# Attention scores on all 128 rows: q stacked high over low, and q padded with zeros

## Chip, cores and metric
The kernel runs on one core of a Trainium2 chip. The metric is the device time of one execution in microseconds (us); lower is better. The engines named below are TensorE (PE; its weight loads are listed apart as PEld), VectorE (DVE), ScalarE (ACT), GpSimd (POOL) and SyncE (SP, which issues the DMAs).

## The reference, cut to what matters
Two blocks of two layers each run one after the other on a sequence of 256 tokens with 1024 columns. Everything is float32. Both blocks contain softmax attention with heads of 64 columns. In the first block 16 query heads share 2 key heads, each query block of 128 tokens sees a band of up to 256 keys, and a sink joins the sum:

```python
def swa_sink_branch(q_in, k_in, v_in, positions, sinks):
    ...
    scores = jnp.einsum('bnqhgd,bnkhd->bnhgqk', qb, kw) * (SW_HEAD_DIM ** -0.5)
    ...
    p = jnp.exp(scores - m)
    probs = p / (jnp.sum(p, axis=-1, keepdims=True) + jnp.exp(sink - m))
    o = jnp.einsum('bnhgqk,bnkhd->bnqhgd', probs.astype(vw.dtype), vw)
```

In the second block there are two streams of 256 tokens, the context stream c and the latent stream h. Each has 6 query heads that share 2 key heads (kind a, `gqa_attention`) and 6 heads with keys of their own (kind b). The latent stream attends to its own keys and to those of the context, 512 in all; in kind b a bias that also holds the mask is added to the scores of its own 256 keys. The last layer computes attention for the latent stream alone.

```python
def gqa_attention(q, k, v):
    ...
        s = jnp.einsum('bqhgd,bkhd->bhgqk', qi, k).astype(jnp.float32) * scale
```

Around the attention stand RMS norms, rotary embedding, a gated delta rule (first block), short convolutions (second block), gates and large feed-forward layers.

## The kernel before
**Matmuls.** Weights stream in by DMA (`wtile`, line 239). Each is split into a high part, rounded to float32r by ACT (line 256), and a low part, the rest, by DVE (line 257). A product is three float32r matmuls: high by high, high by low, low by high (`mm3`, line 260). `lin_a` and `lin_b` loop these over tiles, and `split_psum` (line 229) makes the two parts from a PSUM result. Attention itself runs on plain float32 operands; PE executes such a matmul as two instructions, a weight load with each. Helpers record ACT, DVE tensor and DVE scalar-tensor operations under lines 210, 198 and 201.

**The order of the work.** The program is written as one sequence and a scheduler orders each engine's queue by priority. `weave` (line 566) interleaves softmax groups: three are active, and each round the newest issues its scores, the one before it its transposes, and the oldest its product with the values. `tick` (line 349) spreads the matrix-vector work of the modulation (`ada_steps`, DVE, lines 310 to 324) over other work at a lower priority.

**One softmax group** (`softmax_group`, line 494). Its heads' scores go to one PSUM bank (line 514). DVE finds the maximum (line 520, or with a mask lines 526 and 530), ACT computes the exponentials and their sums (line 538), PE transposes the probabilities (line 551), ACT or DVE copies them out (lines 554, 556), PE multiplies them with the values (line 562), and ACT scales the result (line 564).

**First block** (`attention1`, line 643). After the rotary embedding, the two key heads are each written twice side by side into `kd` (line 659), so that a PE transpose (line 663) puts a copy of the key head into rows 0 to 63 and another into rows 64 to 127 of `kT`. Two query heads lie side by side in 128 columns, so a transpose (line 670) puts the even head into rows 0 to 63 and the odd one into rows 64 to 127 of `qT`; ACT scales by 1/8 as it copies. A score matmul takes one head's 64 rows (line 681). A group holds heads of one parity: four heads by 128 keys for the first token half, two heads by 256 keys for the second.

**Second block.** `mix2` (line 1318) prepares each stream (`prepare`, line 1374): `qk_heads` (line 1234) norms and rotates q and k, then `heads_by_columns` (line 1268) writes `kd`, transposes q (lines 1281 to 1285) and k (lines 1286 to 1291) for both kinds, three heads' pairs at a time. `attend2` (line 1294) builds the groups: two heads with 256 keys each in the context stream, one head with twice 256 keys in the latent stream; heads 0 to 5 of kind a come first, then those of kind b, even and odd in turn. The context stream's groups are woven first, then the latent stream's for both token halves. In the first layer the gate and convolution projections (`conv`, line 1341) are issued before the latent groups, in the last layer after them; the scheduler may draw either forward.

Pools: `ap` holds the attention's tiles (`qT` 2 or 3 buffers, `kT`), `work` holds `w2` (three buffers, shared with evacuations and the modulation), and the PSUM pool for small results has four banks.

Of the kernel before, what the change touches and what calls it, by code (L numbers as in the profile page):

```python
# [9 lines left out]
F32R = mybir.dt.float32r  # L10
# [3 lines left out]
ALU = mybir.AluOpType  # L14
# [3 lines left out]
P = 128  # L18
D = 1024
S = 256  # L20
# [143 lines left out]
class Kern:  # L164
# [329 lines left out]
    def softmax_group(self, ap, heads, sink, out):  # L494


        nc = self.nc
        nh = len(heads)
        nk = sum(p[2] for p in heads[0])
        nb = nk // P  # L500
        biased = heads[0][0][3] is not None
        ncol = len(heads[0]) if biased else 1
        sc = self.t(ap, [P, 512], "sc", bufs=3)
        sc = sc[:, :nh * nk].rearrange("p (h k) -> p h k", h=nh)
        mx = self.t(self.small, [P, nh, 2], "mx", bufs=4)
        nm = self.t(self.small, [P, nh], "nm", bufs=4)
        sums = self.t(self.small, [P, nh, 2], "sums", bufs=4)
        rd = self.t(self.small, [P, nh], "rd", bufs=4)
        ps = self.psum([P, nh, nk])
        src = {}  # L510
        for h, parts in enumerate(heads):
            o = 0
            for i, (q, k, n, bias, _) in enumerate(parts):
                nc.tensor.matmul(ps[:, h, o:o + n], lhsT=q, rhs=k, start=True, stop=True)  # L514
                src[h, i] = (ps[:, h, o:o + n], slice(o, o + n))
                o += n
            if not biased:
                src[h, 0] = (ps[:, h, :], slice(0, nk))
        if not biased:
            nc.vector.tensor_reduce(out=mx[:, :, 0], in_=ps, axis=AX.X, op=ALU.max)  # L520
        else:
            for h, parts in enumerate(heads):
                for i, (_, _, n, bias, _) in enumerate(parts):
                    a, c = src[h, i]
                    if bias is not None:
                        nc.vector.tensor_tensor_reduce(sc[:, h, c], a, bias, scale=1.0, scalar=NEG,
                                                       op0=ALU.add, op1=ALU.max, accum_out=mx[:, h, i:i + 1])
                        src[h, i] = (sc[:, h, c], c)
                    else:
                        nc.vector.tensor_reduce(out=mx[:, h, i:i + 1], in_=a, axis=AX.X, op=ALU.max)  # L530
        other = sink if sink is not None else mx[:, :, 1] if ncol == 2 else None
        if other is not None:
            self.tt(mx[:, :, 0], mx[:, :, 0], other, ALU.max)
        self.ts(nm, mx[:, :, 0], -1.0, ALU.mult)
        for h in range(nh):
            for i in range(ncol):
                a, c = src[h, i]
                self.act(sc[:, h, c], a, AF.Exp, bias=nm[:, h:h + 1], accum_out=sums[:, h, i:i + 1])
        if sink is not None:
            self.tt(sums[:, :, 1], sink, nm, ALU.add)  # L540
            self.act(sums[:, :, 1], sums[:, :, 1], AF.Exp)
        if other is not None:
            self.tt(rd, sums[:, :, 0], sums[:, :, 1], ALU.add)
            nc.vector.reciprocal(rd, rd)
        else:
            nc.vector.reciprocal(rd, sums[:, :, 0])
        yield
        pT = self.t(ap, [P, 4, P], "pT", bufs=2)
        ps = self.psum([P, 4, P])
        for b in range(nh * nb):  # L550
            nc.tensor.transpose(ps[:, b, :], sc[:, b // nb, (b % nb) * P:(b % nb + 1) * P], self.ident)  # L551
        self.flip += 1
        if self.flip % 2:
            nc.scalar.copy(pT[:, :nh * nb, :], ps[:, :nh * nb, :])
        else:
            nc.vector.tensor_copy(pT[:, :nh * nb, :], ps[:, :nh * nb, :])
        yield
        po = self.psum([P, nh, 64])
        for h, parts in enumerate(heads):
            vs = [v for p in parts for v in p[4]]  # L560
            for kb, v in enumerate(vs):
                nc.tensor.matmul(po[:, h, :], lhsT=pT[:, h * nb + kb, :], rhs=v, start=kb == 0, stop=kb == nb - 1)  # L562
        for h in range(nh):
            self.act(out[h], po[:, h, :], scale=rd[:, h:h + 1])

    def weave(self, gens, width, gap=1):

# [74 lines left out]

    def attention1(self, l, ap, swt, oh, ol):
        nc = self.nc
        kT = self.t(ap, [P, 2, S], "kT")
        gens = []
        for tb in range(2):
            x = swt[tb][:, 16:16 + 18 * 64].rearrange("p (h d) -> p h d", d=64)
# [12 lines left out]
            ps = self.psum([P, 4, P])  # L661
            for j in range(2):
                nc.tensor.transpose(ps[:, j, :], kdf[:, j * P:(j + 1) * P], self.ident)
            nc.scalar.copy(kT[:, :, tb * P:(tb + 1) * P], ps[:, 0:2, :])
            qT = self.t(ap, [P, 8, P], "qT", bufs=2)
            for b in range(2):
                ps = self.psum([P, 4, P])
                for j in range(4):
                    c = 16 + (b * 4 + j) * P
                    nc.tensor.transpose(ps[:, j, :], swt[tb][:, c:c + P], self.ident)  # L670
                self.act(qT[:, b * 4:b * 4 + 4, :], ps, scale=0.125)
            o = self.t(self.work, [P, D], "xn", bufs=2)
            nk = P * (tb + 1)
            bias = self.band[:, 0:nk] if tb else self.band[:, P:2 * P]
# [1 line left out]
            for h0 in range(0, 16, step):  # L676
                for par in range(2):
                    hs = range(h0 + par, h0 + step, 2)
                    heads = []
                    for h in hs:  # L680
                        r = slice(par * 64, par * 64 + 64)
                        kv = h // 8
                        vs = [swt[kb][:, 1168 + 64 * kv:1232 + 64 * kv] for kb in range(tb + 1)]
                        heads.append([(qT[r, h // 2, :], kT[r, kv, 0:nk], nk, bias, vs)])
                    c = R_SINK + 16 * l + h0 + par
                    sink = self.rows[:, c:c + step - par:2]
                    gens.append(self.softmax_group(ap, heads, sink, [o[:, 64 * h:64 * h + 64] for h in hs]))
# [579 lines left out]

    def heads_by_columns(self, ap, st, pj, qk, tb, kT):

        nc = self.nc  # L1270
        kd = self.t(ap, [P, 4, 64], "kd")
        for d in range(2):
            nc.vector.tensor_copy(kd[:, d::2, :], qk[:, 6:8, :])
        kdf = kd.rearrange("p a d -> p (a d)")
        qf = qk.rearrange("p h d -> p (h d)")
        s = slice(tb * P, (tb + 1) * P)
        qT = None
        if st.full:
            qT = self.t(ap, [P, 6, P], "qT", bufs=3)
            for b in range(2):  # L1280
                ps = self.psum([P, 3, P])
                for j in range(3):
                    src = qf[:, j * P:(j + 1) * P] if b == 0 else pj[:, 384 + j * P:384 + (j + 1) * P]
                    nc.tensor.transpose(ps[:, j, :], src, self.ident)
                self.act(qT[:, 3 * b:3 * b + 3, :], ps, scale=0.125)
        for j0, m in ((0, 2), (2, 3)):
            ps = self.psum([P, 3, P])
            for j in range(m):
                src = kdf[:, j * P:(j + 1) * P] if j0 == 0 else pj[:, 1024 + j * P:1024 + (j + 1) * P]
                nc.tensor.transpose(ps[:, j, :], src, self.ident)  # L1290
            nc.vector.tensor_copy(kT[:, j0:j0 + m, s], ps[:, :m, :])
        return qT

    def attend2(self, ap, qT, keys, bias, tb):

        o = self.t(self.work, [P, D], "xn", bufs=2)
        heads = {}
        for att in range(2):
            for h in range(6):
                r = slice((h % 2) * 64, (h % 2) * 64 + 64)  # L1300
                kb, v0 = (h // 3, 896 + 64 * (h // 3)) if att == 0 else (2 + h // 2, 1408 + 64 * h)
                parts = []
                for i, (kT, pjs) in enumerate(keys):
                    b = bias[:, h, :] if att == 1 and i == 0 and bias is not None else None
                    parts.append((qT[r, 3 * att + h // 2, :], kT[r, kb, :], S, b, [p[:, v0:v0 + 64] for p in pjs]))
                c = 384 * att + 64 * h
                heads[6 * att + h] = (parts, o[:, c:c + 64])
        per = 2 // len(keys)
# [9 lines left out]
    def mix2(self, l, h, c, nx, then):  # L1318
# [6 lines left out]
        with ExitStack() as es:  # L1325
            xt, ot = nx.x, {}
            with ExitStack() as es2:
# [44 lines left out]
                    ot[st.name] = [self.t(pool, [P, KB, S], tag, F32R, bufs=2) for _ in range(2)]  # L1372

                def prepare(st):
                    kT[st.name] = self.t(ap, [P, 5, S], "kT", bufs=2)
                    for tb in range(2):
                        qk = self.qk_heads(l, ap, st, pj[st.name][tb], tb, True if st is h else None, gtab)
                        qT[st.name, tb] = self.heads_by_columns(ap, st, pj[st.name][tb], qk, tb, kT[st.name])
# [107 lines left out]
```

## Time and profile before

| what | us |
|---|---|
| median of 3 runs | 2934.77 |
| the three runs | 2934.77, 2903.42, 2937.95 |
| the profiled execution | 2933.71 |
| its span, first to last instruction | 2931.9 |
| PE busy in the span | 2863.6 |
| DVE busy | 2110.2 |
| ACT busy | 1320.1 |

The profile is of one execution. Busy time of PE counts from a matmul's start to its modelled end, and matmuls overlap; the distance from one start to the next is the pace. In a timeline a row is one instruction or several alike in a row: start, length, engine, line, operation, written tile and read tiles, shapes, count, and in brackets the idle time before it with what ended it. A form such as 64*128 says that a matmul uses 64 rows and 128 columns of the array. [...]

### The profile page before, as it was taken

What the parts mean: (1) busy time and instruction counts of PE and PEld (TensorE: products, weight loads), DVE (VectorE), ACT (ScalarE), POOL (GpSimd) and SP (SyncE); (2) the same over time, 40 slices, a digit from 0 to 9 for tenths busy, and PEclk for the clock granted to TensorE, in tenths of its full rate; (3) what the DMA queues carried; (4) which work ended last, traced back from release to release, by engine and by line L of the source; (5) the groups of instructions that cost most, each with busy time, mean ns of one, the idle gap of its engine ahead of it and who ended that gap; (6) DMA issues with size and microseconds to landing.
All of it is one profiled execution on the core that took longest, in us unless ns stands there. A gap on an engine that the chain in (4) does not pass through costs nothing.

```text
span 2931.9 us, 51176 instructions
## 1 busy us (share of the span) xinstructions
PE 2863.6 (98%) x19840; PEld 2636.8 (90%) x19840; DVE 2110.2 (72%) x5011; ACT 1320.1 (45%) x2599; POOL 0.2 (0%) x4
## 2 busy tenths in 40 slices
PE   8999999999999999999999999999999999999998
PEld 7999989789988898998978889999999989887897
DVE  7888667988876778777798769777685634764664
ACT  6555464465545554332343555332353323544543
POOL 0000000000000000000000000000000000000000
PEclk9999999999999999999999999999999999987999
DMA  6532557655235665545445224545535433230564
GB/s 221 176 101 73 160 174 236 208 156 172 81 103 171 196 200 170 156 140 154 138 123 160 69 80 125 164 141 154 159 114 160 137 101 107 86 124 12 148 192 143
DMA packets 443908, 416.76 MB, mean 142 GB/s; under 512 B 18320, under 2 KB 383760, under 8 KB 443664
## 3 DMA queue, kind: packets, MB, share of 16 engines
q1 hardware_dynamic: 443664, 413.49, 46.4%
q8 instruction: 156, 2.56, 0.3%
q14 instruction: 88, 0.72, 0.1%
HBM read 412.37 MB, written 1.05 MB: 141 GB/s over the span
## 4 chain that ended last, share of the span: by engine, by line
PE 85%; DVE 7%; DMA 4%; ACT 3%; issue 2%; SPq 0%; DVEq 0%; ACTq 0%
PE mm L265 22%; PE mm L264 22%; PE mm L266 22%; PE sm L514 3%; PE sm L562 3%; DVE lo L198 2%; PE sm L551 2%; DMA araw<-in_w_ada 1%; PE sm L795 1%; DVE acc L201 1%; PE sm L790 1%; ACT hi L210 1%; PE sm L264 1%; PE sm L265 1%; PE sm L266 1%
## 5 line engine op out<-in xcount | busy, mean ns | idle before, releaser
L198 DVE TENSOR_TENSOR lo<-raw,hi 128x1024 fp32r<-128x1024 f32 (+2 forms) x628 | 750.1, 1206 | 339.9 <-ACT hi L210 338.6
L210 ACT ACTIVATE hi<-raw 128x1024 fp32r<-128x1024 f32 (+2 forms) x628 | 647.3, 1046 | 740.0 <-PE mm L265 317.0
L264 PE MATMUL mm<-xTh,hi 128*128 128x256 f32 x2336 | 656.5, 281 | 3.0 <-ACT xTh L210 3.0
L265 PE MATMUL mm<-xTh,hi 128*128 128x256 f32 x2336 | 654.0, 280 | 0.8 <-DVE xTh L201 0.8
L266 PE MATMUL mm<-xTh,lo 128*128 128x256 f32 x2336 | 650.6, 279 | 0.0
L265 PEld LDWEIGHTS mm<-xTh,hi 128*128 128x128 f32 x2336 | 442.9, 190 | 4.7 <-issue 3.3
L264 PEld LDWEIGHTS mm<-xTh,hi 128*128 128x128 f32 x2336 | 438.8, 188 | 5.0 <-ACT xTh L210 3.5
L266 PEld LDWEIGHTS mm<-xTh,lo 128*128 128x128 f32 x2336 | 438.9, 188 | 1.4 <-issue 1.3
L201 DVE SCALAR_TENSOR_TENSOR acc<-araw,csil,acc 128x256 f32<-128x256 f32 x896 | 390.5, 478 | 67.2 <-DMA araw<-in_w_ada 64.7
L264 PE MATMUL mm<-hi,hid 128*128 128x512 f32 x872 | 340.7, 391 | 0.0
L266 PE MATMUL mm<-hi,hid 128*128 128x512 f32 x872 | 340.0, 390 | 0.0
L265 PE MATMUL mm<-lo,hid 128*128 128x512 f32 x872 | 339.7, 390 | 0.0
L264 PE MATMUL mm<-xTc,hi 128*128 128x256 f32 x1104 | 308.9, 280 | 0.0
L265 PE MATMUL mm<-xTc,hi 128*128 128x256 f32 x1104 | 306.6, 278 | 0.0
L266 PE MATMUL mm<-xTc,lo 128*128 128x256 f32 x1104 | 305.3, 277 | 1.1 <-DVE lo L198 1.1
L265 PEld LDWEIGHTS mm<-xTc,hi 128*128 128x128 f32 x1104 | 208.6, 189 | 0.7 <-issue 0.3
L266 PEld LDWEIGHTS mm<-xTc,lo 128*128 128x128 f32 x1104 | 206.5, 187 | 1.3 <-DVE lo L198 1.3
L264 PEld LDWEIGHTS mm<-xTc,hi 128*128 128x128 f32 x1104 | 206.6, 187 | 0.3
L266 PEld LDWEIGHTS mm<-hi,hid 128*128 128x128 f32 x872 | 164.0, 188 | 34.3
L264 PEld LDWEIGHTS mm<-hi,hid 128*128 128x128 f32 x872 | 164.0, 188 | 33.2
L265 PEld LDWEIGHTS mm<-lo,hid 128*128 128x128 f32 x872 | 163.9, 188 | 33.3 <-DVE lo L198 0.2
L264 PE MATMUL mm<-hi,xTh 128*128 128x256 f32 (+3 forms) x512 | 178.3, 350 | 4.4 <-ACT xTh L1147 2.8
(315 smaller groups left out, 4631.7 us busy)
## 6 DMA issues: line engine op xcount, KB each, us to landing
raw<-in_ffn_wi SPq DMA_DIRECT2D x352, 256.0 KB, 3.7
araw<-in_w_ada SPq DMA_DIRECT2D x288, 256.0 KB, 3.0
raw<-in_w_ff SPq DMA_DIRECT2D x128, 512.0 KB, 4.2
raw<-in_w_in SPq DMA_DIRECT2D x116, 512.0 KB, 4.0
raw<-in_ffn_wo SPq DMA_DIRECT2D x88, 512.0 KB, 4.1
raw<-in_w_o SPq DMA_DIRECT2D x40, 512.0 KB, 3.3
raw<-in_w_in SPq DMA_DIRECT2D x24, 432.0 KB, 4.6
raw<-in_w_up_sw SPq DMA_DIRECT2D x16, 512.0 KB, 3.6
```

Source lines behind the costliest of these rows:

```text
L198: self.nc.vector.tensor_tensor(out=out, in0=a, in1=b, op=op)
L201: self.nc.vector.scalar_tensor_tensor(out=out, in0=a, scalar=s, in1=b, op0=op0, op1=op1)
L210: self.nc.scalar.activation(out, a, func, **kw)
L264: mm(ps, lhsT=ah, rhs=bh, start=first, stop=False)
L265: mm(ps, lhsT=ah, rhs=bl, start=False, stop=False)
L266: mm(ps, lhsT=al, rhs=bh, start=False, stop=last)
L514: nc.tensor.matmul(ps[:, h, o:o + n], lhsT=q, rhs=k, start=True, stop=True)
L551: nc.tensor.transpose(ps[:, b, :], sc[:, b // nb, (b % nb) * P:(b % nb + 1) * P], self.ident)
L562: nc.tensor.matmul(po[:, h, :], lhsT=pT[:, h * nb + kb, :], rhs=v, start=kb == 0, stop=kb == nb - 1)
L790: nc.tensor.matmul(ps[:, i, :], lhsT=LT[:, i, :], rhs=Dm[:, i, :], start=True, stop=True)
L795: nc.tensor.matmul(ps[:, i, :], lhsT=DT[:, i, :], rhs=M[:, i, :], start=True, stop=True)
```

## The change
Heads that share keys (all of the first block, kind a of the second): a new helper, `stack_q`, writes each head's q as a stack of 128 rows, the float32r high part in its own 64 rows and the low part in the other 64. The keys, already present in both halves, are split into `kh` and `kl` (float32r). A score is then two accumulating float32r matmuls over 128 rows, the stack times `kh` and the stack times `kl`. Heads with keys of their own (kind b): q goes into `qz`, a tile of 128 rows in which GpSimd fills the other head's 64 rows with zeros; the score is one float32 matmul of 128 rows against the pair of key heads in `kb`. `kd` is now written after the q transposes and takes a buffer of `w2`. Edits that only renumber the entries of a part are left out.

```diff
@@ softmax_group
-            for i, (q, k, n, bias, _) in enumerate(parts):
-                nc.tensor.matmul(ps[:, h, o:o + n], lhsT=q, rhs=k, start=True, stop=True)
+            for i, (qk, n, bias, _) in enumerate(parts):
+                for m, (q, k) in enumerate(qk):
+                    nc.tensor.matmul(ps[:, h, o:o + n], lhsT=q, rhs=k, start=m == 0, stop=m == len(qk) - 1)
...
+    def stack_q(self, qs, ps, scale):
+        for d in range(2):
+            own, other = slice(64 * d, 64 * d + 64), slice(64 - 64 * d, 128 - 64 * d)
+            self.act(qs[own, d::2, :], ps[own], scale=scale)
+            self.stt(qs[other, d::2, :], ps[own], scale, qs[own, d::2, :], ALU.mult, ALU.subtract)
...
@@ attention1
-        kT = self.t(ap, [P, 2, S], "kT")
+        kh, kl = (self.t(ap, [P, 2, S], x, F32R) for x in ("kh", "kl"))
...
-            nc.scalar.copy(kT[:, :, tb * P:(tb + 1) * P], ps[:, 0:2, :])
-            qT = self.t(ap, [P, 8, P], "qT", bufs=2)
+            s = slice(tb * P, (tb + 1) * P)
+            self.split_psum(kh[:, :, s], kl[:, :, s], ps[:, 0:2, :])
+            qs = self.t(ap, [P, 16, P], "qs", F32R, bufs=2)
...
-                self.act(qT[:, b * 4:b * 4 + 4, :], ps, scale=0.125)
+                self.stack_q(qs[:, b * 8:b * 8 + 8, :], ps, 0.125)
...
-                        r = slice(par * 64, par * 64 + 64)
...
-                        heads.append([(qT[r, h // 2, :], kT[r, kv, 0:nk], nk, bias, vs)])
+                        qk = [(qs[:, h, :], k[:, kv, 0:nk]) for k in (kh, kl)]
+                        heads.append([(qk, nk, bias, vs)])
...
@@ heads_by_columns
-        kd = self.t(ap, [P, 4, 64], "kd")
-        for d in range(2):
-            nc.vector.tensor_copy(kd[:, d::2, :], qk[:, 6:8, :])
-        kdf = kd.rearrange("p a d -> p (a d)")
+        kh, kl, kb = kT
...
-            qT = self.t(ap, [P, 6, P], "qT", bufs=3)
+            q = self.t(ap, [P, 6, P], "qs", F32R, bufs=3), self.t(ap, [P, 2, 3, P], "qz", bufs=3)
+            for d in range(2):
+                nc.gpsimd.memset(q[1][64 - 64 * d:128 - 64 * d, d], 0.0)
...
-                self.act(qT[:, 3 * b:3 * b + 3, :], ps, scale=0.125)
+                if b == 0:
+                    self.stack_q(q[0], ps, 0.125)
+                else:
+                    for d in range(2):
+                        r = slice(64 * d, 64 * d + 64)
+                        self.act(q[1][r, d], ps[r], scale=0.125)
+        kd = self.t(self.work, [P, 4, 64], "w2", bufs=3)
+        for d in range(2):
+            nc.vector.tensor_copy(kd[:, d::2, :], qk[:, 6:8, :])
+        kdf = kd.rearrange("p a d -> p (a d)")
...
-            nc.vector.tensor_copy(kT[:, j0:j0 + m, s], ps[:, :m, :])
-        return qT
+            if j0 == 0:
+                self.split_psum(kh[:, :, s], kl[:, :, s], ps[:, :m, :])
+            else:
+                nc.vector.tensor_copy(kb[:, :, s], ps[:, :m, :])
+        return q
...
@@ attend2
-                    parts.append((qT[r, 3 * att + h // 2, :], kT[r, kb, :], S, b, [p[:, v0:v0 + 64] for p in pjs]))
+                    qk = [(qT[0][:, h, :], k[:, h // 3, :]) for k in kT[:2]] if att == 0 else [(qT[1][:, h % 2, h // 2, :], kT[2][:, h // 2, :])]
+                    parts.append((qk, S, b, [p[:, v0:v0 + 64] for p in pjs]))
...
@@ mix2, prepare
-                    kT[st.name] = self.t(ap, [P, 5, S], "kT", bufs=2)
+                    kT[st.name] = [self.t(ap, [P, 2, S], x, F32R, bufs=2) for x in ("kh", "kl")] + [self.t(ap, [P, 3, S], "kb", bufs=2)]
```

## Rows read from the trace of the kernel before

**Rows 1.** The page: busy time by engine, and the chain of waits by engine.
```profile
PE 2863.6 (98%) x19840; PEld 2636.8 (90%) x19840; DVE 2110.2 (72%) x5011; ACT 1320.1 (45%) x2599; POOL 0.2 (0%) x4
...
PE 85%; DVE 7%; DMA 4%; ACT 3%; issue 2%; SPq 0%; DVEq 0%; ACTq 0%
```
**Rows 2.** Table by stage: length, busy PE, PEld, DVE, ACT, POOL, granted clock, DMA.
```profile
50.00:97.00 47.00, 46.97 (x337) 40.04 (x335) 37.84 (x163) 33.64 (x118) 0.00 (x0) 1.00 0.39 115
614.00:661.00 47.00, 46.99 (x344) 40.72 (x342) 39.78 (x174) 34.34 (x121) 0.00 (x0) 1.00 0.41 124
1608.00:1641.00 33.00, 32.28 (x218) 26.49 (x216) 19.94 (x67) 19.89 (x76) 0.00 (x0) 1.00 0.08 29
1672.00:1750.00 78.00, 77.87 (x456) 62.16 (x456) 55.06 (x178) 42.24 (x122) 0.00 (x0) 1.00 0.29 91
2620.00:2677.00 57.00, 55.59 (x199) 44.70 (x199) 19.27 (x70) 18.08 (x58) 0.00 (x0) 0.50 0.11 33
```
**Rows 3.** The scores' line: instructions, ns min/median/max, and matmuls of each form.
```profile
L514 PE MATMUL sm<-kT,qT x368: 272/376/792, 51.4 to 2703.1; 64*128 64x256 f32 x152, 64*128 64x128 f32 x32
```
**Rows 4.** PE's timeline, first block's attention in the second layer.
```profile
631.42 1.00 PE L562 MATMUL sm<-swt,pT 128*128 128x64 f32 x8
632.35 1.13 PE L514 MATMUL sm<-kT,qT 64*128 64x256 f32 x4
633.41 0.39 PE L265 MATMUL mm<-xTh,hi 128*128 128x256 f32 x1
633.64 0.28 PE L266 MATMUL mm<-xTh,lo 128*128 128x256 f32 x1
633.76 0.28 PE L264 MATMUL mm<-xTh,hi 128*128 128x256 f32 x1
```
**Rows 5.** PE's timeline: 128-column scores, and float32 of 128 rows in the delta rule.
```profile
614.59 1.71 PE L514 MATMUL sm<-kT,qT 64*128 64x128 f32 x16
...
260.79 2.12 PE L771 MATMUL sm<-kq 128*128 128x256 f32 x8
262.75 0.50 PE L795 MATMUL sm<-M,DT 128*128 128x128 f32 x3
```
**Rows 6.** PE's timeline, last layer's latent attention: front, one round, end.
```profile
2614.70 1.14 PE L514 MATMUL sm<-kT,qT 64*128 64x256 f32 x8
...
2617.67 0.66 PE L551 MATMUL sm<-cst,sc 128*128 128x128 f32 x4 [1.40 <-ACT sc L210]
2618.26 1.13 PE L514 MATMUL sm<-kT,qT 64*128 64x256 f32 x4
...
2621.73 2.07 PE L514 MATMUL sm<-kT,qT 64*128 64x256 f32 x4
2623.74 1.11 PE L551 MATMUL sm<-cst,sc 128*128 128x128 f32 x4
2624.64 1.81 PE L562 MATMUL sm<-pj,pT 128*128 128x64 f32 x8
2626.38 2.07 PE L514 MATMUL sm<-kT,qT 64*128 64x256 f32 x4
...
2674.12 1.11 PE L551 MATMUL sm<-cst,sc 128*128 128x128 f32 x4 [1.41 <-ACT sc L210]
...
2677.87 1.13 PE L514 MATMUL sm<-kT,qT 64*128 64x256 f32 x4
```
**Rows 7.** Groups of instructions by line and shape: count, busy us, mean ns.
```profile
L201 DVE SCALAR_TENSOR_TENSOR xTh<-sm,hg,xTh 128x512 fp32r<-128x512 f32 x8 | 5.4, 741 | 0.0
L210 ACT ACTIVATE qT<-sm 128x384 f32<-128x384 f32 x12 | 5.2, 488 | 1.3 <-PE sm L1284 1.3
L526 DVE CUSTOM_DVE_ANT_0 sc<-sm,bias 128x256 f32<-128x256 f32 x24 | 10.2, 425 | 26.6 <-PE sm L514 26.5
L210 ACT ACTIVATE sc<-sc,nm 128x256 f32<-128x256 f32 x56 | 28.1, 504 | 18.6 <-DVE rd L544 10.0 <-DVE nm L205 8.4
```
**Rows 8.** PE's timeline, front of the context stream: first transposes after the scores.
```profile
1611.47 0.44 PE L551 MATMUL sm<-cst,sc 128*128 128x128 f32 x2 [0.72 <-ACT sc L210]
```

More of the change, by code (lines that the diff above doesn't have):

```diff
@@ L498, in softmax_group @@
         nh = len(heads)
-        nk = sum(p[2] for p in heads[0])
+        nk = sum(p[1] for p in heads[0])
         nb = nk // P
-        biased = heads[0][0][3] is not None
+        biased = heads[0][0][2] is not None
         ncol = len(heads[0]) if biased else 1
@@ L522, in softmax_group @@
             for h, parts in enumerate(heads):
-                for i, (_, _, n, bias, _) in enumerate(parts):
+                for i, (_, n, bias, _) in enumerate(parts):
                     a, c = src[h, i]
@@ L559, in softmax_group @@
         for h, parts in enumerate(heads):
-            vs = [v for p in parts for v in p[4]]
+            vs = [v for p in parts for v in p[3]]
             for kb, v in enumerate(vs):
@@ L1270, in heads_by_columns @@
         nc = self.nc
-        kd = self.t(ap, [P, 4, 64], "kd")
-        for d in range(2):
-            nc.vector.tensor_copy(kd[:, d::2, :], qk[:, 6:8, :])
-        kdf = kd.rearrange("p a d -> p (a d)")
+        kh, kl, kb = kT
         qf = qk.rearrange("p h d -> p (h d)")
         s = slice(tb * P, (tb + 1) * P)
-        qT = None
+        q = None
         if st.full:
-            qT = self.t(ap, [P, 6, P], "qT", bufs=3)
+            q = self.t(ap, [P, 6, P], "qs", F32R, bufs=3), self.t(ap, [P, 2, 3, P], "qz", bufs=3)
+            for d in range(2):
+                nc.gpsimd.memset(q[1][64 - 64 * d:128 - 64 * d, d], 0.0)
             for b in range(2):
@@ L1299, in attend2 @@
             for h in range(6):
-                r = slice((h % 2) * 64, (h % 2) * 64 + 64)
-                kb, v0 = (h // 3, 896 + 64 * (h // 3)) if att == 0 else (2 + h // 2, 1408 + 64 * h)
+                v0 = 896 + 64 * (h // 3) if att == 0 else 1408 + 64 * h
                 parts = []
```

## The prediction
> **What bounds the kernel now.** I read the busy times and the chain of waits first: TensorE (PE) is busy 98% of the span and carries 85% of the chain [rows 1]. [...] Five stretches hold the attention scores (line 514): the first block's attention in both layers (50 to 97 and 614 to 661 us), the second block's context stream (1608 to 1641) and latent stream (1672 to 1750) in its first layer, and the latent stream in its second (2620 to 2677, with a rest up to 2704). In all of them PE is 97 to 100% busy, so PE is the bound; but in the first block's two, VectorE (DVE) is busy 37.8 and 39.8 of 47 us, close behind. And one differs: from 2620 to 2677 the granted clock is 0.50 (1.2 GHz), in the others 1.00 (2.4 GHz) [rows 2].
>
> The times are those of the profiled execution: span 2931.9, with 1.8 us around it 2933.7. The median of the three runs is 2934.8, so terms can be taken from it directly. One of the three is 2903.4, 31 us shorter; I come back to that.
>
> **One block of scores.** There are 184 score matmuls, and each float32 one is two instructions, 368 in all, on 64 of the 128 rows; 152 of the matmuls have 256 columns, 32 have 128 [rows 3]. In the timeline a block of four (one round's scores) starts at 632.35 and the next matmul at 633.41: 1.06 us. That next one, a float32r matmul of 128 rows, is followed only 0.23 later by its successor, where this form then runs at 0.12 (633.64 to 633.76): the change of form costs another 0.11. A block costs 1.17 [rows 4].
>
> **The change, heads with shared keys** (all 64 score matmuls of the first block, 60 of the second's 120). Two float32r instructions of 128 rows replace two float32 instructions of 64: the same count. At 0.115 to 0.12, four make 0.47, and 0.09 for entering float32r after a float32 or transpose block (taken a little below the 0.11 above) 0.56. A 256-column block saves 1.17 - 0.56 = 0.6 us. Of 128 columns the trace has no float32r matmul. The float32 ones of 128 columns, at the front of a first-block attention, took 1.71 for 16, 0.107 each [rows 5]. Below, 0.115 is the pace of 64-column float32 matmuls, 0.93 for eight [rows 4], which looks like a floor per weight load; above, 0.245 is the pace of a float32 instruction with 128 rows and 256 columns, eight from 260.79 to 262.75 [rows 5]. I take 0.115, the row nearest in width: no gain or loss. At the upper end 32 per layer would cost 32 x 0.13 = 4.2 us a layer.
>
> **Heads with own keys** (60 matmuls). They stay float32 and get 128 rows, half of them zeros. At 0.245 [rows 5] four make 0.98 against 1.17: 0.2 saved, all of it change of form.
>
> **What is lost.** At the front of the last attention eight score instructions take 1.14 (2614.70), as long as four elsewhere [rows 4, 6]: two groups on opposite row halves ran side by side. Two such fronts are as good as unchanged (8 x 0.115 = 0.92), so I drop about 1 us at each front. [...]
>
> PE's saving by stage: first block, eight 256-column groups a layer, 8 x 0.6 and some 0.7 of changes of form, 5.5 a layer; context stream 6 x 0.6 + 6 x 0.2 - 1 = 3.8; latent stream, first layer, 12 x 0.6 + 12 x 0.2 - 1 = 8.6; second layer, the ten groups after 2677, 4 x 0.6 + 6 x 0.2 = 3.6.
>
> **The added work.** stack_q makes of one ACT evacuation two and adds two DVE operations (stt). From the nearest row, an stt from PSUM to float32r of 128x512 at 0.741 [rows 7]; with 384 columns, by share, 0.56. The stacked tiles have 64 partitions; the records here show cost by columns, so I take the full price (half of it is the lower bound). First block: 4 x 2 x 0.741 and two subtractions for k of half the columns, some 0.4 each, give DVE 6.7 us a layer. There DVE had 7 to 9 us free of 47 [rows 2], and PE's part shrinks to 41.5: DVE, 44.5 to 46.5, is then the longer one, unless its modulation work slips out of the stretch. So of 5.5 I take 1.5 a layer, 3 for both (bounds -1 and 5.5 a layer).
> In the second block three preparations get, per token half, 2 x 0.56 of DVE and two more ACT evacuations of 0.49 [rows 7]; kh and kl replace one DVE copy by an ACT copy and a subtraction. The second token half's keys release the first scores. In their way come about 1.1 (DVE), 0.5 and 0.4 (ACT): 2 us per stage, of which projection matmuls cover a little: -5 in all (bounds 0 and -8). Each new stt also waits some 0.5 for ACT's copy; behind it in DVE's queue stand the subtractions that split weights, for which the covering projection matmuls wait: part of the same 5. The 12 zero fills go to GpSimd, which has nothing else (4 instructions, [rows 1]); their price isn't in the trace, but the tile is wanted several us later; I take nothing. If a fill took 2 us, it would still be under the chain of norm, rope and transposes. kd, now behind the q transposes and in one of three shared buffers, delays k by the stacking already counted.
>
> **The half-clock stretch** is the largest term. The clock fell after the block at 2618.26 (1.13, still 2.4 GHz) and before that at 2621.73 (2.07); just ahead PE had idled 1.40 us (before 2617.67). It stayed at 1.2 GHz through eleven rounds like the one shown, each with a 64-row block of 2.0 us. It was at 2.4 GHz again in the block at 2677.87 (1.13), after some 6 us without a 64-row block: transposes, value matmuls and an idle of 1.41 [rows 6]. A full-clock round needs 1.06 + 0.59 (transposes, 2617.67 to 2618.26) + 0.93 = 2.58 [rows 4, 6]; here it is 4.65 (2621.73 to 2626.38). I read it as: the 64-row blocks keep the clock down once a gap has lowered it. The change leaves none. A fall at the front is then still likely (the first exponentials are no faster), but it should be brief.
> New stage, from 2614.70 to 2677.87 (63.2 now; a front of two groups up to 2618.26, twelve rounds, a tail of some 3.6): front 3.6 as now; six shared-key rounds, 0.56 + 0.59 + 0.93 = 2.1 each; between a group's scores and its transposes the trace has 1.83 (2615.84 to 2617.67) [rows 6], which PE's other work just covers. Six own-key rounds: PE 2.5; their chain is longer, mask and maximum 0.43 each and two exponentials of 0.50 [rows 7], with small steps and semaphores some 2.6: 2.6 each. Tail 2, a brief half clock 2.5. Sum 3.6 + 12.6 + 15.6 + 2 + 2.5 = 36, saved 27.
>
> **Sum.** 3 (first block) + 2/3 of 16 (3.8 + 8.6 + 3.6; the rest goes into waits for the softmax), 11, + 27 - 5 = 36: 2933.7 - 36 = **2898 us**. Against the run of 2903 it would be a gain of 5 only; I suspect that this run kept its clock, since the stage at full clock would be 3.6 + 12 x 2.6 + 2 = 37, and 63.2 - 37 = 26 is most of the 31.
>
> **Rivals.**
> 1. *The clock stays low in the last stage* (it also falls where chains idle, and transposes and value matmuls remain). Then, with 0.90 and 1.74 for transposes and value matmuls [rows 6] and the scores at twice their time, rounds cost 0.94 + 0.09 + 0.90 + 1.74 = 3.7 and 1.96 + 0.90 + 1.74 = 4.6; stage 3.6 + 22.2 + 27.6 + 3.6 = 57, saved 6: 2933.7 - (3 + 11 + 6 - 5) = 2919. For it: PE is quicker, so idles longer. Against: the recovery at 2677 needed only the instructions that remain.
> 2. *All of PE's saving is real* and preparation is covered: 11 + 16 + 29.5 (no brief half clock): 2877. Against: DVE in the first block.
> 3. *Slower: the clock falls in the context stream too.* Its front has the same shape and now less PE work to bridge the first exponentials; before, PE idled 0.72 there [rows 8], after, about 1.5 with preparation longer. It decides from a gap like the 1.40 that preceded the fall. Twelve rounds at about 4.1 instead of 2.5, some 20 us, and as much again in part of the latent stream (10), with the last stage as in rival 1: 2919 + 30 = 2949. Against: projection matmuls stand between the rounds there.
> 4. *The half clock is chance, not the rows*: some runs have it, some not, before and after. Then the median may fall on either side, 2898 or 2919.
>
> **How the numbers follow.** Forecast 0.54, rival 1 0.17, rival 2 0.16, rival 3 0.06, rival 4 0.07. The range, 2870 to 2926, takes in the 128-column price, DVE's bounds and rivals 1 and 2, and leaves out rival 3 and the far ends. A measurement of this kernel can tell about 2% (58.7 us) from no change. Faster by more, below 2876, needs rival 2 with a little more: 0.17; slower by more, 2993, needs rival 3 in more than two stages: 0.03; within 0.80.
>
> **What would show it.** Right: no 64-row form at line 514; shared-key blocks of four near 0.47 and own-key blocks near 0.98; a clock of 1.00 in most of the last stage and its length near 36; DVE above 90% in the first block's attention. Wrong: a clock of 0.50 through that stage, or 128-column instructions near 0.245, or new PE idle at each stage's front of over 3 us.

## The result and the profile after

The kernel after takes 2884.78 us (median of four runs, 2882.61 to 2889.78); the kernel before, run beside it, 2933.13 (2903.42 to 2937.95). The ratio is 0.9864, 95% interval 0.9816 to 0.9912: 1.4% faster. The profiled execution took 2885.26 us, its span is 2883.5. The forecast of 2898 was 13 us too long, and its range holds the result.

The page, where [rows 1] stood: the count of PE's instructions is the same, PE is 59 us less busy, DVE and ACT a little more; POOL's 12 added zero fills took 5.0 us.

```profile
PE 2804.2 (97%) x19840; PEld 2608.6 (90%) x19840; DVE 2131.3 (74%) x5043; ACT 1333.5 (46%) x2627; POOL 5.2 (0%) x16
...
PE 82%; DVE 9%; DMA 4%; ACT 4%; issue 2%; SPq 0%; DVEq 0%; ACTq 0%
```

The table by stage, where [rows 2] stood (length, busy PE, PEld, DVE, ACT, POOL, granted clock, DMA):

```profile
50.00:97.00 47.00, 45.17 (x377) 43.01 (x375) 44.06 (x176) 36.87 (x126) 0.00 (x0) 1.00 0.40 120
614.00:661.00 47.00, 42.63 (x350) 41.36 (x351) 43.08 (x175) 37.08 (x128) 0.00 (x0) 0.96 0.39 118
1604.00:1636.00 32.00, 32.00 (x261) 31.20 (x260) 24.88 (x85) 21.55 (x78) 0.82 (x2) 1.00 0.17 54
1664.00:1740.00 76.00, 73.14 (x480) 63.54 (x481) 60.50 (x197) 43.46 (x121) 0.00 (x0) 0.98 0.36 112
2598.00:2635.00 37.00, 33.22 (x248) 28.87 (x246) 26.28 (x89) 22.93 (x69) 0.00 (x0) 1.00 0.23 72
```

Two things are to be seen. In the first block's two stretches PE is no longer full: 1.8 and 4.4 us of 47 idle, with DVE at 44.1 and 43.1. And the last stretch is at a clock of 1.00 and is 37 us long where it was 63. The 0.96 of the second layer is a short fall that is new: PE idled 1.86 us at the front there, the clock was at 0.50 from 621.6 to 625.0, and then at 1.00 again.

```profile
621.16 0.33 PE L552 MATMUL sm<-cst,sc 128*128 128x128 f32 x1 [1.86 <-ACT sc L210]
```

The scores' line, where [rows 3] stood: no 64-row form is left.

```profile
L515 PE MATMUL sm<-kh,qs x124: 273/283/455, 53.1 to 2641.9; 128*128 128x256 f32 x92, 128*128 128x128 f32 x32
...
L515 PE MATMUL sm<-kb,qz x120: 377/379/435, 1608.7 to 2657.6; 128*128 128x256 f32 x120
```

PE's timeline of the last layer's latent attention, where [rows 6] stood: front, shared-key rounds, an own-key round.

```profile
2598.61 0.39 PE L515 MATMUL sm<-kh,qs 128*128 128x256 f32 x1 [0.36 <-ACT kh L210]
...
2602.14 0.27 PE L266 MATMUL mm<-xTh,lo 128*128 128x256 f32 x1
2602.62 0.66 PE L552 MATMUL sm<-cst,sc 128*128 128x128 f32 x4 [0.20 <-ACT sc L210]
2603.03 0.36 PE L515 MATMUL sm<-kh,qs 128*128 128x256 f32 x1
...
2603.59 0.60 PE L552 MATMUL sm<-cst,sc 128*128 128x128 f32 x4
...
2605.07 0.36 PE L515 MATMUL sm<-kh,qs 128*128 128x256 f32 x1
...
2606.09 0.66 PE L552 MATMUL sm<-cst,sc 128*128 128x128 f32 x4 [0.29 <-ACT sc L210]
...
2607.39 0.36 PE L515 MATMUL sm<-kh,qs 128*128 128x256 f32 x1
...
2610.64 0.66 PE L552 MATMUL sm<-cst,sc 128*128 128x128 f32 x4 [0.55 <-ACT sc L210]
...
2611.97 1.08 PE L515 MATMUL sm<-kb,qz 128*128 128x256 f32 x4
2613.21 0.66 PE L552 MATMUL sm<-cst,sc 128*128 128x128 f32 x4 [0.15 <-ACT sc L210]
...
2614.54 1.08 PE L515 MATMUL sm<-kb,qz 128*128 128x256 f32 x4
...
2634.93 0.36 PE L515 MATMUL sm<-kh,qs 128*128 128x256 f32 x1
```

At the front, projection matmuls now run until 2602.4, so PE idles 0.20 us before the first transposes, not 1.40, and the clock stays at 1.00 through this stage. Three shared-key rounds (2605.07 to 2611.97) take 2.3 each, with 0.3 to 0.55 us in two of them in which PE waits for the exponentials; the one own-key round shown takes 2.57, of which 0.15 is such a wait.

Where the time went, from the start of the first score instruction to the start of the last in each stage, by five of the profiles (the last three columns are kernels of the experiments):

| stage, us | before | after | all 64 rows | all padded | first block padded |
|---|---|---|---|---|---|
| first block, layer 1 | 43.5 | 40.3 | 47.1 | 38.4 | 38.4 |
| first block, layer 2 | 42.6 | 41.1 | 49.5 | 38.2 | 38.2 |
| context stream | 29.1 | 28.2 | 32.1 | 26.0 | 28.2 |
| latent, first layer | 73.6 | 70.0 | 77.2 | 66.8 | 68.5 |
| latent, last layer | 88.4 | 59.0 | 71.1 | 60.0 | 59.0 |
| sum | 277.1 | 238.6 | 277.1 | 229.3 | 232.3 |

The stages give 38.5 of the 48 us between the two spans. The four stretches between them sum to 2374.5 before and 2365.9 after, but a second profile of the kernel before, taken in the experiments, has 2366.8: in sum those 9 us are mostly what the same kernel varies by.

### The profile page after: what moved, and what is told of

Read it like the earlier page. It is cut to its first block, busy times and chain, and to the rows that moved or that the text cites. A ratio compares the mean times of both kernels' runs of the same rounds, so it can differ in the third digit from the quotient of the medians.

```text
span 2883.5 us, 51232 instructions
## 1 busy us (share of the span) xinstructions
PE 2804.2 (97%) x19840; PEld 2608.6 (90%) x19840; DVE 2131.3 (74%) x5043; ACT 1333.5 (46%) x2627; POOL 5.2 (0%) x16
## 4 chain that ended last, share of the span: by engine, by line
PE 82%; DVE 9%; DMA 4%; ACT 4%; issue 2%; SPq 0%; DVEq 0%; ACTq 0%
PE mm L265 22%; PE mm L264 22%; PE mm L266 22%; PE sm L563 2%; DVE lo L198 2%; PE sm L515 2%; DVE acc L201 2%; PE sm L552 1%; DMA araw<-in_w_ada 1%; PE sm L805 1%; PE sm L800 1%; ACT hi L210 1%; PE sm L264 1%; PE sm L265 1%; PE sm L266 1%
```

## The experiments

**All scores on 64 rows again.** Stacking, splitting and padding stay, but each matmul reads its head's own 64 rows (the low part of q, and the zeros, are left out of the products).

```diff
-    qk = [(qs[:, h, :], k[:, kv, 0:nk]) for k in (kh, kl)]
+    r = slice(h % 2 * 64, h % 2 * 64 + 64)
+    qk = [(qs[r, h, :], k[r, kv, 0:nk]) for k in (kh, kl)]
```

(and the same in `attend2`, for both kinds.)

> The changed kernel with all its added work, but every score matmul takes only the 64 rows of its own head (for shared keys the low part of q, which lies in the other 64 rows, is left out of the scores). Theory A (blocks on 64 rows keep the clock down once a gap has lowered it): the last latent stage is at a clock of 0.50 for most of its rounds, some 55 us long instead of 35, and each block costs 0.1 to 0.2 us more for the change of form; 2912 to 2922 us. Rival B (the clock depends on the idle gap at the stage's front and on PE's pace, both as in the changed kernel here, not on rows): clock 1.00 there, 2885 to 2900 us. Rival C (chance): runs of either kind in one kernel.

Measured 2924.54 (2913.76 to 2930.39), ratio 1.001 [0.9977, 1.0043], just above theory A's 2912 to 2922. With the rows the whole gain goes, float32r or not. It was not only the clock: its run of 2913.76 had a mean granted clock of 0.993, like the kernel after, and is still some 29 us above it. What theory A said of the clock did not come in the run that was traced: PE idled only 0.37 us at the last stage's front, and 33 us of rounds with 64-row blocks ran at 1.00 before 17 us at half clock:

```profile
2632.00:2665.00 33.00, 31.03 (x211) 25.43 (x211) 22.45 (x79) 19.95 (x59) 0.00 (x0) 1.00 0.23 72
2665.00:2682.00 17.00, 16.18 (x61) 13.33 (x61) 6.09 (x17) 5.19 (x14) 0.00 (x0) 0.51 0.00 1
```

So 64-row blocks alone did not lower the clock in those 33 us, behind a front idle of 0.37 us.

**Only the own-key heads on 64 rows.** The same edit for kind b alone.

> The changed kernel, but the heads with own keys take only their own 64 rows (nothing is left out: the other rows hold zeros). Theory A: blocks of these heads cost 1.06 to 1.17 again instead of 0.73 to 0.92, and if a gap in the own-key half of the last latent stage lowers the clock there, it stays at 0.50 to that half's end: 2888 to 2905 us. Rival B: clock 1.00 throughout, only the change of form, 2887 to 2893 us.

Measured 2896.88 (2890.65 to 2900.93), ratio 0.9899: 8 us above the kernel after as repeated below, 12 above its first median. For 30 blocks that is 0.26 to 0.40 a block; the prediction had 0.2. By stage its profile gives less: context stream, latent stream and last layer take 30.7, 70.7 and 61.5 us, against 28.2, 68.5 and 59.0 in the second profile of the kernel after, 7.2 in all or 0.24 a block.

**Padding alone.** The kernel before, with q of every head padded with zeros to 128 rows in the manner of `qz`, one float32 matmul each, and no stacking.

```diff
-    qT = self.t(ap, [P, 8, P], "qT", bufs=2)
+    qT = self.t(ap, [P, 2, 8, P], "qT", bufs=2)
+    for d in range(2):
+        nc.gpsimd.memset(qT[64 - 64 * d:128 - 64 * d, d], 0.0)
...
-    heads.append([(qT[r, h // 2, :], kT[r, kv, 0:nk], nk, bias, vs)])
+    heads.append([(qT[:, par, h // 2, :], kT[:, kv, 0:nk], nk, bias, vs)])
```

> The kernel before, with q of every head padded with zeros to 128 rows; scores stay float32, no split, no stacking (GpSimd fills, ACT evacuates twice). PE has the pace of before and the same front with its idle gap, only the rows differ. Theory A: clock back at 1.00 within a few us of the last latent stage's front, stage of 36 to 40 us, and 0.1 to 0.3 us less per block: 2893 to 2905 us. Rival B (gap and pace decide): clock 0.50 in that stage as before, 2915 to 2930 us. Rival C: either, from run to run.

Measured 2880.50 (2878.59 to 2882.82), ratio 0.9851 [0.9797, 0.9904]: at least as fast as the change, and below the 2893 to 2905 expected, without float32r scores and without the 21 us of DVE work. The table by stage of this kernel shows where:

```profile
614.00:661.00 47.00, 46.98 (x382) 45.55 (x382) 42.46 (x157) 34.04 (x112) 0.00 (x0) 1.00 0.41 122
```

PE is full there, as before [rows 2], but in the same 47 us it issues 382 instructions where the kernel before issued 344 and the kernel after 350. At the last stage's front the idle was not the same as before, as the expectation had it, but half as long:

```profile
2592.86 0.66 PE L551 MATMUL sm<-cst,sc 128*128 128x128 f32 x4 [0.74 <-ACT sc L210]
```

The eight score instructions took 1.96 us there and not 1.14, which fills part of the old idle, and the clock stayed at 1.00 (every later block of the stage took 1.03 to 1.08). So this run prices the 64 rows, but does not show what they do to a clock that has fallen.

**The kernel before, again.**

> The kernel before, unchanged, to see its runs one by one. Theory A: runs near 2933 us have a mean clock near 0.984, a run near 2903 (if one comes) near 0.994, the difference being the half-clock stretch of the last latent stage. Rival C the same, and then in about a third of the runs. If a run near 2903 came with a clock of 0.984, its 31 us are something else.

Measured 2930.61, ratio 1.0018. In the experiments the kernel before ran 59 times, these ten included, and its runs fall in two groups: 26 of 2903 to 2917 us, with a mean granted clock of 0.990 to 0.996, and 33 of 2927 to 2953, with 0.977 to 0.987. Both traced runs are of the second group. In the first profile of the kernel before, the half-clock stretch lasts 58 us (2619.6 to 2677.6), which alone lowers the mean clock of a 2932 us run by 0.010: without it, that run's 0.984 would be 0.994, as in the first group. By this estimate, the stretch is there in somewhat more than half of the runs. The run traced here (2946.87, clock 0.978) has it twice:

```profile
2614.00:2656.00 42.00, 42.00 (x148) 33.54 (x149) 14.20 (x57) 14.06 (x47) 0.00 (x0) 0.50 0.10 29
...
2662.45 0.66 PE L551 MATMUL sm<-cst,sc 128*128 128x128 f32 x4 [1.41 <-ACT sc L210]
...
2665.00:2713.00 48.00, 48.00 (x154) 36.68 (x152) 13.52 (x51) 13.54 (x42) 0.00 (x0) 0.50 0.00 0
```

The clock came back in between (1.00 from 2657 to 2662), after transposes and value matmuls of two rounds had run with no 64-row block between them. It fell again behind an idle of 1.41 us.

Of the kernels with 128 rows, 36 runs (the change and the padded ones, all but the one that stacks twice) all had 0.991 to 0.997.

**First block padded, second as in the change; and the reverse.** The first block takes the edit above, the second keeps the stack; then the other way about.

> The changed kernel, but the first block's attention keeps float32 scores with q padded by zeros to 128 rows, in place of the stacking (no split of its k, no stt); the second block is as in the change. If the stacking of the first block costs what it saves or more because DVE is the longer engine there, this is 5 to 12 us below the changed kernel: 2873 to 2880 us. If float32r's pace pays in the first block, it is 5 to 11 us above: 2890 to 2896 us.

> The other half: first block stacked as in the change, second block with zeros and float32 for all heads. If the stacking in the second block pays (its PE time 0.56 a block against 0.92, 30 blocks, less the longer preparation), this is 3 to 8 us above the changed kernel: 2888 to 2893 us. If its preparation costs as much as it saves: 2883 to 2887 us. Padding everywhere stood at 2880.5 us, so this and the run with the first block padded should lie on opposite sides of it or add up to it: first block's step plus second block's step = -4.

**The change with each subtraction of the stack issued twice,** and **the change again,** on the same chip:

```diff
     self.stt(qs[other, d::2, :], ps[own], scale, qs[own, d::2, :], ALU.mult, ALU.subtract)
+    self.stt(qs[other, d::2, :], ps[own], scale, qs[own, d::2, :], ALU.mult, ALU.subtract)
```

> The changed kernel with every stt of stack_q issued twice (same result): 28 more DVE operations, 16 of 0.684 and 12 of 0.555, 17.6 us of DVE. If the added DVE work stands on the path in the first block and in the preparations, 8 to 15 us above the changed kernel: 2893 to 2900 us. If it is hidden behind matmuls: within 3 us of it.

> The changed kernel, unchanged, beside the three others on the same chip: 2880 to 2890 us, mean clock 0.992 to 0.995 in every run. A run with a clock near 0.984 would say that the half-clock stretch can come without blocks on 64 rows.

Measured: change again 2889.18; first block padded 2875.62 (ratio 0.9852 [0.9801, 0.9903]), 13.6 less; second block padded 2890.08, 0.9 more; stack twice 2903.84, 14.7 more. In the first block the stack loses to padding; twice the stacking lengthens the kernel by about its added DVE time (17 us by the page). So DVE is on the path there. Part of the 14.7 is clock: the runs that stack twice had 0.985 to 0.991, and the one at 0.991 (2901.39) stands 12 above the change's at 0.991. PE's timeline of that kernel shows how the two hang together, in the first block and at the last layer's front:

```profile
657.21 0.44 PE L552 MATMUL sm<-cst,sc 128*128 128x128 f32 x2 [0.99 <-ACT sc L210]
...
660.70 0.56 PE L552 MATMUL sm<-cst,sc 128*128 128x128 f32 x2 [1.51 <-ACT sc L210]
...
2617.94 1.12 PE L552 MATMUL sm<-cst,sc 128*128 128x128 f32 x4 [2.30 <-ACT sc L210]
```

and its table by stage, around the two:

```profile
660.00:680.00 20.00, 17.38 (x81) 16.71 (x82) 13.30 (x50) 9.42 (x35) 0.00 (x0) 0.52 0.39 115
2617.00:2630.00 13.00, 11.94 (x55) 11.65 (x56) 8.94 (x21) 5.67 (x17) 0.00 (x0) 0.50 0.13 42
```

After idles of 0.99 and 1.51 us, and of 2.30, the clock fell to 0.50, and with 128-row blocks and further idles among them it was back 13 to 20 us later. That suggested the next pair.

**An idle forced at the front of the last layer's latent attention,** in the padded kernel and in the kernel before:

```diff
-    nc.vector.tensor_reduce(out=mx[:, :, 0], in_=ps, axis=AX.X, op=ALU.max)
+    for _ in range(8 if getattr(self, "lag", 0) > 0 else 1):
+        nc.vector.tensor_reduce(out=mx[:, :, 0], in_=ps, axis=AX.X, op=ALU.max)
+    self.lag = getattr(self, "lag", 0) - 1
...
+    self.lag = 2 if last else 0
     self.weave(gens, 3)
```

> The kernel before with q padded to 128 rows for every head (no stacking), and at the front of the last layer's latent attention the maximum of the first two groups taken 8 times instead of once (7 more of 0.69 us each, 4.8 us a group), so that TensorE must idle there for some 4 to 9 us. Theory (an idle lowers the clock, and only rounds with 64-row blocks keep it down): granted clock 0.50 after the idle for some 10 to 15 us (as in the run that stacks twice, where it fell after an idle of 2.30 and was back 13 us later), then 1.00 for the rest of the stage; 9 for the idle and 6 for the clock over the padded kernel's 2880: about 2895 (2888 to 2902). Rival (the rows do not matter; once fallen, the clock stays down through any stage of this kind): 0.50 to the stage's end, about 2880 + 9 + 25 = 2914.

> The kernel before with the same idle forced at the same place; scores on 64 rows. Theory: the clock falls at this front in every run, not only in some, and stays at 0.50 through the rounds with 64-row blocks, some 55 us; so no run near 2905, all of them 2935 to 2950. Rival (a fall is chance, an idle does not bring it): times as scattered as those of before, 2905 to 2950, each some 9 later.

Measured: padded with idle 2888.06 (2885.87 to 2890.06); before with idle 2943.86, no run of ten below 2940.41, while the kernel before beside them had ten of 17 runs under 2912. Timeline of the padded kernel with idle:

```profile
2584.20 1.95 PE L514 MATMUL sm<-kT,qT 128*128 128x256 f32 x8
...
2595.44 1.12 PE L553 MATMUL sm<-cst,sc 128*128 128x128 f32 x4 [9.06 <-ACT sc L210]
2596.35 1.92 PE L514 MATMUL sm<-kT,qT 128*128 128x256 f32 x4
...
2600.00 1.08 PE L514 MATMUL sm<-kT,qT 128*128 128x256 f32 x4
...
2602.57 1.08 PE L514 MATMUL sm<-kT,qT 128*128 128x256 f32 x4
2603.49 0.60 PE L553 MATMUL sm<-cst,sc 128*128 128x128 f32 x4
2603.93 1.00 PE L564 MATMUL sm<-pj,pT 128*128 128x64 f32 x8
2604.77 1.08 PE L514 MATMUL sm<-kT,qT 128*128 128x256 f32 x4
```

and of the kernel before with idle:

```profile
2611.73 1.14 PE L514 MATMUL sm<-kT,qT 64*128 64x256 f32 x8
...
2623.01 1.12 PE L553 MATMUL sm<-cst,sc 128*128 128x128 f32 x4 [9.71 <-ACT sc L210]
2624.06 2.07 PE L514 MATMUL sm<-kT,qT 64*128 64x256 f32 x4
...
2688.91 2.07 PE L514 MATMUL sm<-kT,qT 64*128 64x256 f32 x4
...
2693.21 1.05 PE L553 MATMUL sm<-cst,sc 128*128 128x128 f32 x4
2694.20 1.13 PE L514 MATMUL sm<-kT,qT 64*128 64x256 f32 x4
```

with its table by stage:

```profile
2623.00:2693.00 70.00, 68.58 (x235) 54.02 (x236) 24.39 (x84) 21.45 (x67) 0.00 (x0) 0.50 0.09 27
```

The idle was as long in both (9.06 and 9.71). With 128 rows the block at 2596.35 ran at half clock (1.92) and the one at 2600.00 at full (1.08): 5 us after the idle it was over. With 64 rows blocks took 2.07 for 65 us, with PE busy 98% of the time, and 1.13 again from 2694.20, after 2.3 us of projection matmuls (five float32r of 128 rows, left out in the rows). The same shows once more, without a forced idle, near the end of the stage. The kernel before fell behind an idle of 1.41 us and stayed low for the 48 us shown above. The padded kernel with idle fell behind one as long, and its block at 2634.63 was at full clock again:

```profile
2629.27 0.66 PE L553 MATMUL sm<-cst,sc 128*128 128x128 f32 x4 [1.41 <-ACT sc L210]
...
2634.63 1.08 PE L514 MATMUL sm<-kT,qT 128*128 128x256 f32 x4
```

So behind idles of 9.06 and 9.71 us the clock was low in both kernels, for 5 us with 128-row blocks and for 70 with 64-row ones; both halves of the prediction's reading are shown for this stage. The rival, a fall that stays whatever the rows, is refuted. The number of rows in use and the change of form around each 64-row block went together in all these kernels, so which of the two keeps the clock low is not shown. What lets the kernel before keep its clock in the other runs, a shorter idle at this front or something else, was not traced.

The padded kernel with idle is 5.5 us above the padded one beside it (2882.61, below), not the 15 expected, though its last stage is 11.0 us longer (71.0 and 60.0). Where the rest was made up is open.

**Padded everywhere against first block only,** side by side on one chip:

> q padded for every head, a second time, to stand beside the next kernel on the same chip. 2880 as before if chips agree. If stacking pays in the second block (two float32r instructions at 0.115 for two float32 ones at 0.245), the next kernel is faster by 60 x 0.25 / 2 = 5 to 8 us less what stacking costs there.

> First block padded, second block as in the change (stacked for shared keys). If stacking in the second block pays: 2873 to 2877, 4 us or more under the kernel padded everywhere. If it pays nothing: equal within 2 us.

Measured 2882.61 (2876.48 to 2885.20) and 2877.94 (2873.43 to 2880.53). So the stack in the second block was worth 4.7 us here, with ranges that overlap, and 0.9 in the runs above (2890.08 against 2889.18): 1 to 5 us. The first profiles of these two kernels lie between. With the stack, the first layer takes 1.2 us more from the first context score to the last latent one (129.1 and 127.9), and the way from there to the last score of the last layer takes 4.2 less (924.1 and 928.3). The fastest version of all is the one with the first block padded, 2875.62 and 2877.94, ratios 0.9852 and 0.9846; it is 7 to 14 us under the change.

## Why the prediction came out as it did

**The half-clock stretch: right in size, with a cause that is shown but was not the one at work at this front.** From the first score of the stage (2598.61) to the block that answers to 2677.87 (2634.93) it now takes 36.3 us for 63.2; forecast 36, with 27 saved, and 27 were. The clock was 1.00 as the sign demanded. Shared-key rounds took 2.3 (forecast 2.1), the own-key round shown 2.57 (2.6). But the prediction saw a fall at the front that 128-row blocks would end soon, its "brief half clock 2.5". That 2.5 was my estimate; no row gives it. No fall came: the front idled 0.20, not 1.40, and in the kernel with all scores on 64 rows, where it idled 0.37, the clock held for 33 us too. The forced idles show what the prediction reasoned from (low for 5 us with 128-row blocks, for 70 with 64-row ones); in the kernel after this may have mattered behind the 1.86 us in the first block, but not here. The traces give the clock as a share of full speed, 0.50 or 1.00; the prediction's 1.2 and 2.4 GHz stand in no trace.

The term belongs to only part of the runs: the suspicion about the run of 2903 was right, and rival 4 holds for the kernel before and not for the kernel after. It is luck that the median shown for the kernel before lay in the lower-clock group. Beside the last experiments it was 2911.32, and the same change would have looked half as large.

**Everything else: mis-sized.** Against the kernel before's runs that kept their clock (2908.8, the median of the ten beside the last experiments) the change still saves 20 to 24 us; the prediction left 3 + 11 - 5 = 9 for that. The stages outside the half-clock stretch gave 38.5 - 26.9 = 11.6 in the two profiles, near the 14 forecast: two terms failed there, with opposite signs, and nearly cancel. The 13 us by which the total is off lie mostly elsewhere: in the preparations' 5, which did not come, and in 6.7 us from stretches in which nothing was changed (951.2 and 947.4 from the first block's last score to the context's first, 228.8 and 225.9 behind the last score). Such stretches vary as much in one kernel: the former has 946.1 in the second profile of the kernel before.

First, "A block costs 1.17". I priced the change of form from the block and the matmul behind it, 0.11, and missed what stands ahead of it. PE's timeline of the kernel before, a round at full clock late in the last layer:

```profile
2682.82 1.13 PE L514 MATMUL sm<-kT,qT 64*128 64x256 f32 x4
2683.88 0.66 PE L551 MATMUL sm<-cst,sc 128*128 128x128 f32 x4
2684.37 1.00 PE L562 MATMUL sm<-pj,pT 128*128 128x64 f32 x8
2685.30 1.13 PE L514 MATMUL sm<-kT,qT 64*128 64x256 f32 x4
```

2.48 from block to block, against 2.20 in the padded round above (2602.57 to 2604.77): scores 1.06 and 0.92, transposes 0.49 and 0.44, value matmuls 0.93 and 0.84. The last 0.09 was in the 0.93 of [rows 4] all the time, booked as the value matmuls' own pace. A 64-row block thus costs 0.28 more than one of 128 rows that does the same arithmetic in the same number of instructions. Of such blocks of four there are 368 / 4 = 92, which makes 26 us; padding alone saved 27 at equal clock (2908.8 against 2880.5 and 2882.6: 26 to 28). The table agrees: in the four stages that ran at full clock in both kernels, padding saves 5.1 + 4.4 + 3.1 + 6.8 = 19.4 us for 68 blocks, 0.285 each. For own keys the prediction had 0.2. The 0.28 is the price of a 64-row block among 128-row matmuls here, in and out together. That the change of form costs it, and not the 64 rows themselves, is my reading and was not shown apart.

Second, the gain from float32r, 0.4 of the 0.6 a block. The matmuls ran as priced: 0.56 a block behind transposes (2603.03 to 2603.59 in the timeline after), and the 128-column ones at the 0.115 taken:

```profile
53.06 0.30 PE L515 MATMUL sm<-kh,qs 128*128 128x128 f32 x1
...
54.87 0.33 PE L264 MATMUL mm<-xTh,hi 128*128 128x256 f32 x1
```

Sixteen in 1.81 us, 0.113 each, from the first to what follows; whether that pace is the floor per weight load that the prediction guessed at is not shown. But little of it reached the end. In the first block DVE is the longer one, as forecast (94 and 92% busy against the 90 demanded): the stages shrank by 3.2 and 1.5 us, but the first began 1.7 later, behind the stacking, and the stretch between the two grew from 519.7 to 521.8. That stretch is 515.9 to 519.7 in all eight profiles without the stack in this block, and 521.8 to 524.7 in all six with it. So about 1 us is left of the forecast's 3. What the prediction did not ask is what zeros alone would give there: 5.1 and 4.4, with a first score only 0.7 later and no longer stretch between. The stack spent there what the 128 rows had gained. In the last layer's rounds it does pay: in the kernel padded everywhere three shared-key rounds take 2.6 each,

```profile
2595.89 1.08 PE L514 MATMUL sm<-kT,qT 128*128 128x256 f32 x4
...
2603.73 1.08 PE L514 MATMUL sm<-kT,qT 128*128 128x256 f32 x4
```

against 2.3, and that stage is 1.0 us shorter with the stack (59.0 and 60.0 in the table). But both streams of the first layer are shorter with zeros (26.0 and 66.8 against 28.2 and 70.0 after, or 68.5 with the first block padded). That DVE's stacking costs it there too is likely, and was not shown stage by stage. The factor of 2/3 was the right thought; it should have struck the float32r part almost whole and the change of form hardly at all.

**Preparations, -5.** Not seen in sum, and of the other sign where it was forecast. In the first block, which had no such term, the scores come later, as just said. In the second block they come earlier: the latent stream's first score comes 32.7 us after the context's last, for 35.1 before, and the last layer's first score 864.0 us after the latent stream's last, for 868.5. So it is in every profile: 32.4 to 33.0 and 864.0 to 866.1 in the seven with the stack in this block, 35.1 to 35.3 and 867.5 to 868.6 in the seven without. Part of this is that the first score with `kh` starts before `kl` is there (2598.61 above). That `kh` is copied by ACT, where DVE copied the keys before, may be the rest; this was not tested. The price per instruction was near: on 64 partitions the subtraction with 512 columns took 0.684 and the one with 384 0.555, against 0.741 and 0.56 taken, so half the partitions saved next to nothing here.

**Rivals.** 1 and 3 are out: no stage stayed at half clock; the context stream was at 1.00, the latent stream's first layer at 0.98. Rival 2's 2877 is as near to the result as the forecast, and its covered preparation is near what the profiles show, but its other ground, all of PE's saving, is not what happened in the first block. Rival 4 is half true, as said. With the mended prices the sum closes: the eleven rounds of the half-clock stretch and the front belong to its 27, some 80 blocks lie outside it, and 80 x 0.28 = 22; 2933.7 - 27 - 22 = 2885. The padded kernel, which is just that, has 2880 to 2883; the change, with the stack's loss in the first block and its gain in the last layer, 2885 to 2889.

## What to carry to other kernels

Price a change of matmul form over the whole round, from one block to the next, against a kernel that differs in the form alone: here the block itself showed 0.14 of the 0.28 us, and the rest sat in the neighbours' ordinary-looking times. Where a stage has a second engine close behind, take the cheapest edit that removes the cost (here zeros, at no DVE work) before the one that also makes the matmul faster. And where single runs stand apart from the median, compare their mean granted clock before putting a clock term into a forecast for all runs. Three of the long stretches at 0.50 in the kernel before are shown with an idle ahead (1.40 and 1.41 us, 9.71 forced) and 64-row blocks within, so ask which of the two the change removes.

## What the hardware showed that I had not expected

After nearly the same idle (9.06 and 9.71 us), the granted clock was back at 1.00 in 5 us with 128-row blocks, and stayed at 0.50 for 70 us with 64-row blocks between the same transposes and value matmuls. PE's busy time does not tell these two apart, 4.56 of the 5.00 us and 68.58 of the 70.00; the form of the score blocks did. Behind an idle of 0.37 us, 64-row blocks ran at 1.00 for 33 us. Against that, 128 rows are no guarantee: in the kernel that stacks twice the mean clock was 0.52 for 20 us after idles of 0.99 and 1.51 us in the first block.
